# Two U-product steps behind the last scores instead of one early and one ahead of them

## Chip, cores and metric

The kernel runs on one core of a Trainium2 chip. The metric is the device time of one execution in microseconds (us). The engines are TensorE (PE, its weight loads PEld), VectorE (DVE), ScalarE (ACT), GpSimd (POOL) and SyncE (SP, which issues most transfers).

## The reference

One layer of a hybrid backbone for 512 latent tokens of width 1024: a Fourier and recurrent mixer, then the PEER retrieval, which is where the change lies. Every token makes 8 heads x 2 queries, scores 128 sub-keys with each, takes the 16 best of each half, the 16 best of their sums, and uses those experts' rows of two tables of 16384 rows, U and V.

```python
q = (xc @ w_q).reshape(T, PEER_HEADS, 2, PEER_KEY_HALF)
s = jnp.einsum('thpd,hpkd->thpk', q, sub_keys).astype(jnp.float32)
s1, i1 = lax.top_k(s[:, :, 0], PEER_TOPK)
s2, i2 = lax.top_k(s[:, :, 1], PEER_TOPK)
...
sc, pos = lax.top_k(cand, PEER_TOPK)
...
act = jax.nn.gelu(jnp.einsum('thkd,td->thk', u, xc).astype(jnp.float32))
return jnp.einsum('thk,thkd->td', (g * act).astype(xc.dtype), v_tab[idx])
```

## The kernel before

For 352 of the 512 tokens the kernel does not gather rows. It multiplies all of U with the tokens (dense), and later weighs and multiplies with all of V. The products of U come in **steps** of 128 experts (`steps_a`): one step splits a weight tile (ACT makes `whi`, POOL or DVE makes `wlo`), issues 24 matmuls of 128x352 into `ps_pa`, and lets ACT apply the GELU into `act`. A load of 1 MB feeds two steps, and a spill (`Ad<-act`) takes four away. The first 40 steps (numbered 0 to 39 here) are **spilled** ones: their order is that of one generator, and code in the query phase calls `next(spilled)` wherever it wants one more step there, so the calls fix how many steps stand at each place.

The query phase has 16 **blocks** (8 heads x 2 halves). Block k issues 24 matmuls of 128x512 for the query into `ps_ps`, splits the result (`qhi` on ACT, `qlo` on DVE), and then issues the **scores** of the block before it, k - 1: 8 small matmuls (L777, L778) against the split keys `kp` (hi on ACT, lo on POOL), copies on ACT, an addition on POOL (L781), and on DVE the search for the 16 best (`top16`, L764 to L769). After every second block DVE also forms sums of candidates (L792, L794) and searches them. The scores of block 15 come last, behind the loop.

Behind that stands a chain: softmax on DVE and ACT, conversion of positions and indices (`PH`, `IH`), transposes on PE (L884), two gathers by table lookup (`gather_idx`: L897, L900 and L893 on PE, L902 on DVE), with a step after every fourth term, 8 in all. Then come 22 chunks of one-hot products (L958 to L971) with one step each. 10 + 8 + 22 = 40. In the rest of the kernel PE works through the other U groups and all of V.

The tile framework schedules: it builds each engine's queue from the program order and its own cost model, so a step's matmuls may stand earlier than its call. Each engine then works through its queue in order. Weight buffers of the steps (`whi`, `wlo`) are double, so the split of step s + 2 waits for the matmuls of step s.

Of the kernel before, what the change touches and what calls it, by code (L numbers as in the profile page):

```python
# [51 lines left out]
def build(tc, xT, ctxT, c2t, vecs, wm, wu, wf, wg, wgate, wo, wq, keys, u, v, urow, vrow,  # L52
# [12 lines left out]
    def act(o, i, f, bias=None, scale=None, **kw):  # L65
        if bias is not None:
            kw["bias"] = bias
        if scale is not None:
            kw["scale"] = scale
        return S.activation(o, i, f, **kw)  # L70
# [37 lines left out]
    def pst(tag="ps", n=512, dt=F32):  # L108
        return psum.tile([P, n], dt, tag=tag, name="ps_" + tag, bufs={"ps": 5, "pm": 1, "pa": 2}[tag])

    def load(ap, st="", cuts=1):
        t = raws.tile([P, 2048], F32, tag="raw" + st, name="raw")
        n = 2048 // cuts
        for c in range(cuts):
            nc.sync.dma_start(t[:, c * n:(c + 1) * n], ap[:, c * n:(c + 1) * n])
        return t
# [4 lines left out]
    def split(dst, src, lo_eng=None):  # L121
        act(dst[0], src, AF.Copy)
        lo_ins[0] = (lo_eng or V).tensor_tensor(dst[1], src, dst[0].bitcast(F32), op=ALU.subtract).ins  # L123
        return dst

    def split_w(raw, h, lo_eng=None, st=""):
        return split((wspl.tile([P, 1024], F32R, tag="whi" + st, name="whi"),
                      wspl.tile([P, 1024], F32R, tag="wlo" + st, name="wlo")),
                     raw[:, h * 1024:(h + 1) * 1024], lo_eng)

    def mm3(ps, a, b, start, stop):
        PE.matmul(ps, a[0], b[0], start=start, stop=False)  # L132
        PE.matmul(ps, a[0], b[1], start=False, stop=False)  # L133
        PE.matmul(ps, a[1], b[0], start=False, stop=stop)  # L134

    def cut(pair, sl):
        return pair[0][:, sl], pair[1][:, sl]
# [625 lines left out]
    def top16(src, n, vals, idx):  # L763
        V.max(vals[:, 0:8], src)  # L764
        V.max_index(idx[:, 0:8], vals[:, 0:8], src)
        rest = qp.tile([P, n], F32, tag=f"rest{n}", name="rest")
        V.match_replace(rest, vals[:, 0:8], src, -3.4e38)
        V.max(vals[:, 8:16], rest)
        V.max_index(idx[:, 8:16], vals[:, 8:16], rest)  # L769

    def scores(h, p, kp, qT):
        sc = qp.tile([P, T], F32, tag="sc", name="sc")
        for b in range(2):
            ps = pst().rearrange("p (t c) -> p t c", t=2)
            for t in range(2):
                a = cut(qT, slice((2 * b + t) * P, (2 * b + t + 1) * P))
                PE.matmul(ps[:, t], a[0], kp[:, p].rearrange("p c k -> p (c k)"), start=True, stop=False)  # L777
                PE.matmul(ps[:, t, :P], a[1], kp[:, p, 0], start=False, stop=True)  # L778
            sc2 = qp.tile([P, 2, 256], F32, tag="sc2", name="sc2")
            act(sc2, ps, AF.Copy)  # L780
            G.tensor_tensor(sc[:, b * 256:(b + 1) * 256].rearrange("p (t k) -> p t k", t=2),  # L781
                            sc2[:, :, :P], sc2[:, :, P:], op=ALU.add)
        for t4 in range(4):
            top16(sc[:, t4 * P:(t4 + 1) * P], P, M[:, t4, p, h], I[:, t4, p, h])
        if p == 0:
            return
        cand = qp.tile([P, 4, NCAND], F32, tag="cand", name="cand")
        s1 = M[:, :, 0, h]
        s2 = M[:, :, 1, h]
        for a in range(8):  # L790
            n = ROWLEN[a]
            V.tensor_tensor(cand[:, :, START[a]:START[a] + n], s2[:, :, 0:n],  # L792
                            s1[:, :, a:a + 1].to_broadcast([P, 4, n]), op=ALU.add)
        V.tensor_tensor(cand[:, :, 42:50], s1[:, :, 8:16], s2[:, :, 0:1].to_broadcast([P, 4, 8]), op=ALU.add)  # L794
        for t4 in range(4):
            top16(cand[:, t4], NCAND, SC[:, t4, h], PO[:, t4, h])
# [7 lines left out]
    def steps_a(g, lo_eng, done):  # L804

        for w in range(JG // 2):
            raw = load(u[g * (JG // 2) + w], "U" if lo_eng else turn(w))
            for h in range(2):
                wp = split_w(raw, h, lo_by[0] if lo_eng else None, "U" if lo_eng else turn(h))
                ps = pst("pa")  # L810
                for d in range(ND):
                    mm3(ps[:, :TD], cut(wp, slice(d * P, (d + 1) * P)), cut(h2[d], slice(TG, T)),
                        d == 0, d == ND - 1)
                if w % 2 == 0 and h == 0:
                    at = act_tile()
                act(at[:, (2 * w + h) % 4], ps[:, :TD], AF.Gelu_apprx_tanh)
                if w % 2 and h:
                    done(g, w // 2, at)
                yield
# [7 lines left out]
    spilled = itertools.chain.from_iterable(steps_a(g, G, spill) for g in range(NSP))  # L827

    late = None
    for h in range(8):  # L830
        raw = load(wq[h]) if h else None
        kraw = qp.tile([P, 256], F32, tag="kraw", name="kraw")
        nc.sync.dma_start(kraw, keys[h])
        kp = qp.tile([P, 2, 2, P], F32R, tag="kp", name="kp")
        split((kp[:, :, 0], kp[:, :, 1]), kraw.rearrange("p (s k) -> p s k", s=2), G)
        for p in range(2):
            wp = split_w(raw, p, G) if h else wpq[p]
            ps = pst()
            for d in range(ND):
                mm3(ps, cut(wp, slice(d * P, (d + 1) * P)), h2[d], d == 0, d == ND - 1)  # L840
            qT = split((qp.tile([P, T], F32R, tag="qhi", name="qhi"),
                        qp.tile([P, T], F32R, tag="qlo", name="qlo")), ps)
            if late:
                scores(*late)
            if p or h == 0:
                next(spilled)
            late = (h, p, kp, qT)
    next(spilled)
    scores(*late)


    SCv = SC.rearrange("p a h k -> p (a h) k")
# [452 lines left out]
```

## Time and profile before

| | |
|---|---|
| median of 3 runs | 1470.51 us (1467.47 to 1471.3) |
| profiled execution | 1468.34 us, its span 1466.6 us |
| mean granted clock of TensorE | 0.977 of full speed |
| query phase with its first transposes | 251.4 to 413.2 us |
| gathers | 413.2 to 453 us |
| one-hot chunks on PE | 466.9 to 587.9 us |
| products with U, V and row gathers | 600 us to the end |

All stretches below are in us from the span's start. Where an engine's busy time equals a stretch it was never without an instruction there.

### The profile page before, as it was taken

Reading aid. Unit: us, or ns where it says so; the run is one execution under the profiler, and the core shown is the slowest. Engines: PE = TensorE matmul, PEld = TensorE weight load, DVE = VectorE, ACT = ScalarE, POOL = GpSimd, SP = SyncE. Lnnn points to the kernel's source line nnn. Section 1 sums busy time; section 2 is a strip of 40 time slices with the busy share of each in tenths; the row PEclk is TensorE's granted clock in tenths of the full one; section 3 lists DMA queues with packets and bytes.
Section 4 is the critical chain, followed back from the end, with each engine's and each line's share of the span. In section 5 each row is a group of like instructions: output and inputs, shape, how many; then the busy total and the mean of one; then the engine's idle time right before and its main releaser. Section 6 shows DMA issues by size and latency. Waiting matters only on the chain. (4 is left out here: it accounts for less than half of the span.)

```text
span 1466.6 us, 22575 instructions
## 1 busy us (share of the span) xinstructions
PE 1388.5 (95%) x8569; PEld 1286.3 (88%) x8569; DVE 1235.2 (84%) x2184; ACT 613.3 (42%) x881; POOL 680.4 (46%) x462
## 2 busy tenths in 40 slices
PE   6897998999989999999999999999999999899995
PEld 2776765888969999999999999999999999899995
DVE  5577875599986999498998979998898989999973
ACT  4467633434334566533333432424334343243351
POOL 0034163666520000465766746675675766544412
PEclk8899999999999999999999999999999999999998
DMA  8333446331225999999999998999999999999911
GB/s 339 157 115 143 171 174 238 134 114 62 105 79 187 311 293 328 359 380 367 402 358 415 355 373 342 414 382 376 397 369 369 399 348 415 399 410 401 391 39 58
DMA packets 130190, 420.61 MB, mean 287 GB/s; under 512 B 10401, under 2 KB 59809, under 8 KB 106017
## 3 DMA queue, kind: packets, MB, share of 16 engines
q1 hardware_dynamic: 83520, 251.03, 45.9%
q0 software_dynamic: 46560, 168.14, 29.7%
q8 instruction: 67, 1.10, 0.3%
q14 instruction: 43, 0.34, 0.1%
HBM read 385.41 MB, written 33.69 MB: 286 GB/s over the span
## 5 line engine op out<-in xcount | busy, mean ns | idle before, releaser
L70 ACT ACTIVATE whi<-raw 128x1024 fp32r<-128x1024 f32 x296 | 312.8, 1060 | 601.8 <-PE ps_pa L133 301.9
L123 DVE TENSOR_TENSOR wlo<-raw,whi 128x1024 fp32r<-128x1024 f32 x264 | 326.3, 1238 | 44.9 <-ACT whi L70 42.1
L132 PE MATMUL ps_pa<-h2h,whi 128*128 128x352 f32 x1024 | 335.7, 328 | 4.0 <-ACT act L70 4.0
L134 PE MATMUL ps_pa<-h2h,wlo 128*128 128x352 f32 x1024 | 333.6, 326 | 0.3 <-DVE wlo L123 0.3
L133 PE MATMUL ps_pa<-h2l,whi 128*128 128x352 f32 x1024 | 333.2, 325 | 0.0
L1089 POOL DMA_INDIRECT row<-vrow,eidx x128 | 192.8, 1506 | 130.1 <-DVE oacc L1110 100.6
L1089 POOL DMA_INDIRECT row<-urow,eidx x128 | 196.7, 1537 | 120.1 <-DVE row L1096 67.2
L133 PE MATMUL ps_ps<-wl,whi 128*128 128x352 f32 x640 | 207.5, 324 | 0.0
L134 PE MATMUL ps_ps<-wh,wlo 128*128 128x352 f32 x640 | 206.9, 323 | 0.0
L132 PE MATMUL ps_ps<-wh,whi 128*128 128x352 f32 x640 | 206.4, 322 | 0.0
L132 PEld LDWEIGHTS ps_pa<-h2h,whi 128*128 128x128 f32 x1024 | 193.3, 189 | 6.2 <-ACT act L70 4.9
L134 PEld LDWEIGHTS ps_pa<-h2h,wlo 128*128 128x128 f32 x1024 | 193.1, 189 | 1.6 <-DVE wlo L123 0.6
L133 PEld LDWEIGHTS ps_pa<-h2l,whi 128*128 128x128 f32 x1024 | 193.3, 189 | 1.1
L1096 DVE SCALAR_TENSOR_TENSOR row<-row,hrow 128x1024 f32<-128x1024 f32 x128 | 153.6, 1219 | 31.1 <-DMA row<-urow,eidx 30.9
L1110 DVE SCALAR_TENSOR_TENSOR oacc<-row,gw,oacc 128x1024 f32<-128x1024 f32 x127 | 162.4, 1279 | 11.5 <-DMA row<-vrow,eidx 11.1
L133 PEld LDWEIGHTS ps_ps<-wl,whi 128*128 128x128 f32 x640 | 120.3, 188 | 0.0
L134 PEld LDWEIGHTS ps_ps<-wh,wlo 128*128 128x128 f32 x640 | 120.3, 188 | 0.0
L132 PEld LDWEIGHTS ps_ps<-wh,whi 128*128 128x128 f32 x640 | 120.3, 188 | 0.0
L123 POOL TENSOR_TENSOR wlo<-raw,whi 128x1024 fp32r<-128x1024 f32 x32 | 76.6, 2395 | 86.9 <-ACT whi L70 60.0
L133 PE MATMUL ps_pa<-wl,whi 128*128 128x352 f32 x256 | 83.0, 324 | 0.0
L134 PE MATMUL ps_pa<-wh,wlo 128*128 128x352 f32 x256 | 82.7, 323 | 0.0
L132 PE MATMUL ps_pa<-wh,whi 128*128 128x352 f32 x256 | 82.5, 322 | 0.0
(299 smaller groups left out, 2611.7 us busy)
## 6 DMA issues: line engine op xcount, KB each, us to landing
raw<-u SPq DMA_DIRECT2D x64, 1024.0 KB, 7.8
raw<-v SPq DMA_DIRECT2D x64, 1024.0 KB, 8.3
raw<-wm SPq DMA_DIRECT2D x24, 1024.0 KB, 6.1
Gd<-stg SPq DMA_DIRECT2D x22, 1024.0 KB, 6.9
gt<-Gd SPq DMA_DIRECT2D x16, 1408.0 KB, 10.3
raw<-wq SPq DMA_DIRECT2D x8, 1024.0 KB, 4.8
Ad<-act SPq DMA_DIRECT2D x10, 704.0 KB, 5.2
act<-Ad SPq DMA_DIRECT2D x10, 704.0 KB, 6.9
```

The source lines that it names most:

```text
L70: return S.activation(o, i, f, **kw)
L123: lo_ins[0] = (lo_eng or V).tensor_tensor(dst[1], src, dst[0].bitcast(F32), op=ALU.subtract).ins
L132: PE.matmul(ps, a[0], b[0], start=start, stop=False)
L133: PE.matmul(ps, a[0], b[1], start=False, stop=False)
L134: PE.matmul(ps, a[1], b[0], start=False, stop=stop)
L1089: G.indirect_dma_start(out=t, out_offset=None, in_=tab, in_offset=bass.IndirectOffsetOnAxis(ap=e[:, s:s + 1], axis=0))
L1096: ins = V.scalar_tensor_tensor(t, t, 1.0, hr, op0=ALU.mult, op1=ALU.mult, accum_out=dt[:, s:s + 1])
L1110: ins = V.scalar_tensor_tensor(o, t, g[:, s:s + 1], o, op0=ALU.mult, op1=ALU.add)
```

## The change

The call after block 0 goes, and the last two calls stand behind the scores of block 15, where there was one call ahead of them. Blocks still issue one step per head, ten steps are still called by the end of the phase, and everything behind it is unchanged in the code. So step 0 is called after block 1 instead of block 0, step k (1 to 8) one call later, and step 8 and step 9 last.

```diff
             if late:
                 scores(*late)
-            if p or h == 0:
+            if p:
                 next(spilled)
             late = (h, p, kp, qT)
+    scores(*late)
     next(spilled)
-    scores(*late)
+    next(spilled)
```

How it moves instructions on the engines is shown at three places.

On PE, at the first scores (`ps_ps_1983` and `ps_ps_2045` or `ps_ps_2012` are the queries of blocks 0 and 1, `ps_pa` is a step). Before, ahead of the first scores, the tail of step 0 and then 23 matmuls of block 1:

```order
L134 MATMUL ps_ps_1983<-h2h7_1940,wlo_1814 128x512
L132 MATMUL ps_pa_2018<-h2h5_1928,whi_2014 128x352
...
L134 MATMUL ps_pa_2018<-h2h7_1940,wlo_2015 128x352
L133 MATMUL ps_ps_2045<-h2l0_1899,whi_1817 128x512
...
L134 MATMUL ps_ps_2045<-h2h7_1940,wlo_1818 128x512
L777 MATMUL ps_ps_2075<-kp_1980,qhi_2008 128x256
```

Now the queries of blocks 0 and 1 run into each other, the scores follow at once, and step 0 stands behind them:

```order
L134 MATMUL ps_ps_1983<-h2h7_1940,wlo_1814 128x512
L134 MATMUL ps_ps_2012<-h2h3_1916,wlo_1818 128x512
...
L134 MATMUL ps_ps_2012<-h2h7_1940,wlo_1818 128x512
L777 MATMUL ps_ps_2042<-kp_1980,qhi_2008 128x256
...
L133 MATMUL ps_pa_2088<-h2l0_1899,whi_2084 128x352
```

23 of step 0's 24 matmuls moved behind the first scores.

On POOL, at the same place (`wlo` of `raw_2012`, `raw_2082` and `raw_2334` are steps, of `raw_2145` and `raw_2115` blocks 2 and 3). Before:

```order
L716 DMA eyeR_1895<-eye 128x128
L123 TENSOR_TENSOR wlo_2153<-raw_2145,whi_2152 128x1024
L123 TENSOR_TENSOR wlo_2337<-raw_2334,whi_2336 128x1024
L123 TENSOR_TENSOR kp_1980<-kraw_1978,kp_1980 128x2x128
L123 TENSOR_TENSOR kp_2149<-kraw_2147,kp_2149 128x2x128
```

Now:

```order
L716 DMA eyeR_1895<-eye 128x128
L123 TENSOR_TENSOR wlo_2123<-raw_2115,whi_2122 128x1024
L123 TENSOR_TENSOR kp_1980<-kraw_1978,kp_1980 128x2x128
L123 TENSOR_TENSOR kp_2119<-kraw_2117,kp_2119 128x2x128
L123 TENSOR_TENSOR wlo_2231<-raw_2115,whi_2230 128x1024
```

One split instead of two stands ahead of the low part of the keys, `kp`, for which the first scores wait.

On ACT, at the end of the phase, where every step has one `act` row (`sc2` are the copies of scores). Before:

```order
L70 ACTIVATE sc2_3622<-ps_ps_3617 128x512
L70 ACTIVATE sc2_3630<-ps_ps_3625 128x512
L70 ACTIVATE whi_3866<-raw_3864 128x1024
L70 ACTIVATE act_3688<-ps_pa_3663 128x352
L70 ACTIVATE whi_3916<-raw_3864 128x1024
L70 ACTIVATE act_3688<-ps_pa_3694 128x352
L70 ACTIVATE sc2_3726<-ps_ps_3721 128x512
L70 ACTIVATE sc2_3734<-ps_ps_3729 128x512
L70 ACTIVATE whi_3969<-raw_3967 128x1024
L70 ACTIVATE act_3688<-ps_pa_3870 128x352
L70 ACTIVATE whi_4020<-raw_3967 128x1024
L70 ACTIVATE act_3688<-ps_pa_3920 128x352
```

Now:

```order
L70 ACTIVATE sc2_3591<-ps_ps_3586 128x512
L70 ACTIVATE sc2_3599<-ps_ps_3594 128x512
L70 ACTIVATE whi_3765<-raw_3732 128x1024
L70 ACTIVATE act_2995<-ps_pa_3630 128x352
L70 ACTIVATE sc2_3663<-ps_ps_3658 128x512
L70 ACTIVATE sc2_3671<-ps_ps_3666 128x512
L70 ACTIVATE whi_3866<-raw_3864 128x1024
L70 ACTIVATE act_2995<-ps_pa_3738 128x352
L70 ACTIVATE whi_3916<-raw_3864 128x1024
L70 ACTIVATE act_2995<-ps_pa_3769 128x352
```

Between the scores of blocks 14 and 15 stands one step (7), where two stood (8 and 9). Behind the scores of block 15 there were steps 10 and 11, and now there are 8 and 9. In PE's queue 300 step matmuls stood ahead of the first transpose (L884): steps 0 to 11 and 12 matmuls of step 12. Now it is 253: steps 0 to 9 and 13 of step 10. From the transposes of the gathers' results (L927) on, the order on PE is the same in both, so that the 47 matmuls stand between L884 and there. On DVE the split `qlo` of block 15's query keeps its place in the queue.

## Rows read from the trace of the kernel before

**Rows 1.** The page: busy us of each engine (share of the span) and instructions.
```profile
PE 1388.5 (95%) x8569; PEld 1286.3 (88%) x8569; DVE 1235.2 (84%) x2184; ACT 613.3 (42%) x881; POOL 680.4 (46%) x462
```

**Rows 2.** Stretches: length, then busy us of each engine; behind them the granted clock.
```profile
core 0: us, PE busy (x) PEld busy (x) DVE busy (x) ACT busy (x) POOL busy (x), PEclk, DMA share, GB/s
251.36:256.48 5.12, 5.12 (x12) 4.01 (x13) 5.12 (x9) 3.19 (x5) 0.00 (x0) 0.50 0.05 8
...
283.50:406.28 122.78, 122.78 (x663) 108.95 (x661) 121.61 (x786) 48.95 (x79) 74.81 (x57) 1.00 0.26 94
406.28:413.18 6.90, 0.00 (x1) 0.01 (x1) 6.77 (x40) 1.09 (x2) 1.50 (x1) 0.78 0.67 256
413.18:416.90 3.72, 3.72 (x21) 3.72 (x22) 3.14 (x9) 3.12 (x5) 0.00 (x0) 0.50 0.02 4
...
420.50:453.00 32.50, 32.50 (x182) 23.48 (x179) 25.02 (x44) 8.80 (x14) 8.22 (x4) 1.00 0.24 87
453.00:467.00 14.00, 14.00 (x90) 13.68 (x89) 8.31 (x11) 4.66 (x8) 0.00 (x0) 1.00 0.68 236
467.00:587.00 120.00, 119.85 (x1159) 112.15 (x1158) 119.97 (x106) 71.99 (x126) 0.00 (x0) 1.00 0.99 301
```

**Rows 3.** Waits of PE, 240 to 600 us: in total, times, longest.
```profile
PE ps_ps L884 <- DVE PH L872: 6.9, 1, 6.9
```

**Rows 4.** Waits of DVE, 284 to 412.5 us.
```profile
DVE M L764 <- POOL sc L781: 0.4, 1, 0.4
```

**Rows 5.** Timeline of PE ahead of its hole: start, duration, instruction.
```profile
405.80 0.32 PE L133 MATMUL ps_pa<-h2l,whi 128*128 128x352 f32 x1
405.96 0.32 PE L134 MATMUL ps_pa<-h2h,wlo 128*128 128x352 f32 x1
```

**Rows 6.** Timeline of PE around the first scores and at the second.
```profile
268.83 0.28 PE L777 MATMUL ps_ps<-kp,qhi 128*128 128x256 f32 x1
...
269.70 0.38 PE L132 MATMUL ps_pa<-h2h,whi 128*128 128x352 f32 x1
...
279.18 0.28 PE L777 MATMUL ps_ps<-kp,qhi 128*128 128x256 f32 x1
```

**Rows 7.** Timeline of POOL, 258 to 284 us.
```profile
263.13 4.76 POOL L123 TENSOR_TENSOR wlo<-raw,whi 128x1024 fp32r<-128x1024 f32 x2 [12.71 <-ACT whi L70]
267.85 1.43 POOL L123 TENSOR_TENSOR kp<-kraw,kp 128x256 fp32r<-128x256 f32 x2
```

**Rows 8.** Timeline of DVE at the second search for the best.
```profile
283.48 0.49 DVE L764 MAX8 M<-sc 128x8 f32<-128x128 f32 x2 [2.01 <-POOL sc L781]
```

**Rows 9.** Timeline of PE at step 8 and the last scores.
```profile
387.85 0.38 PE L132 MATMUL ps_pa<-h2h,whi 128*128 128x352 f32 x1
...
395.58 0.28 PE L777 MATMUL ps_ps<-kp,qhi 128*128 128x256 f32 x1
```

**Rows 10.** Timeline of DVE: the last query's split.
```profile
394.74 0.68 DVE L123 TENSOR_TENSOR qlo<-ps_ps,qhi 128x512 fp32r<-128x512 f32 x1
```

**Rows 11.** DVE's groups of 389.5 to 392, then of 404.5 to 408.3 us: count, busy, mean ns.
```profile
L792 DVE TENSOR_TENSOR cand<-M 128x8 f32<-128x8 f32 (+5 forms) x8 | 1.0, 174 | 0.0
...
L792 DVE TENSOR_TENSOR cand<-M 128x8 f32<-128x8 f32 (+5 forms) x8 | 3.0, 428 | 0.0
```

**Rows 12.** Timeline of DVE: the last round of additions begins.
```profile
404.78 0.28 DVE L792 TENSOR_TENSOR cand<-M 128x32 f32<-128x32 f32 x2
```

**Rows 13.** Timeline of POOL, 404.5 to 409 us.
```profile
405.43 2.35 POOL L123 TENSOR_TENSOR wlo<-raw,whi 128x1024 fp32r<-128x1024 f32 x1 [1.44 <-ACT whi L70]
```

**Rows 14.** The page: issues of U loads, KB each, us to landing.
```profile
raw<-u SPq DMA_DIRECT2D x64, 1024.0 KB, 7.8
```

**Rows 15.** Timeline of ACT ahead of the first one-hot product.
```profile
459.94 1.06 ACT L70 ACTIVATE whi<-raw 128x1024 fp32r<-128x1024 f32 x1 [2.43 <-PE ps_pa L133]
```

**Rows 16.** Timeline of DVE at the first one-hot product.
```profile
461.03 1.23 DVE L123 TENSOR_TENSOR wlo<-raw,whi 128x1024 fp32r<-128x1024 f32 x1 [1.55 <-ACT whi L70]
462.18 1.22 DVE L958 TENSOR_TENSOR X<-io,i1T 128x2048 f16<-128x2048 f16 x1
```

## The prediction

> **What bounds the kernel now.** The page comes first: PE is busy for 95% of the span and DVE for 84% [rows 1], so an average does not tell which of them sets the pace where the change lies. The table of stretches does. From the second scores to the end of the query phase PE is busy for all of 122.78 us, and DVE for 121.61 [rows 2]. DVE's list of waits has 0.4 us in that time [rows 4]. Both are full, and each feeds the other: DVE waits for no scores because it is behind, PE for no split query. Then comes a hole: PE has nothing for 6.90 us, which its waits put down to `PH`, the last positions that DVE finds [rows 2, 3]. After that PE is without a break again, through the gathers (32.50 of 32.50 us) and up to the first one-hot products (14.00 of 14.00) [rows 2]. In the one-hot chunks DVE sets the pace (119.97 of 120.00), but its first one-hot product stands in its queue behind the split of a step at 461.03, which waited for ACT at 459.94, which waited for PE to free a weight buffer [rows 15, 16]. So the start of that stage too is PE's.
>
> What the reader is to take from this: from the query phase on, PE's amount of work is fixed (40 steps, 16 blocks, the same lookups and chunks), and PE has few holes. The change can win or lose by what it does to PE's idle time, and nearly by that alone.
>
> **The change part by part.** First the unit. Step matmuls start 0.16 us apart [rows 5], so a step is 24 x 0.16 = 3.84 us of PE. The 8 score matmuls take 269.70 - 268.83 = 0.87 us until the next may start [rows 6].
>
> *The step that leaves the start.* 23 of its matmuls stood ahead of the first scores, at 268.83. Without them PE has block 1's query done 3.7 us earlier, at about 265.1. But the scores also need the low part of the keys from POOL. Before, POOL made two splits in 4.76 us from 263.13 on and then the two keys in 1.43 us [rows 7]. Now one split stands ahead: 263.13 + 2.4 + 0.7 = 266.2, and the scores start at about 266.3, which is 2.5 us earlier, with PE idle for 1.2 us. The second scores, behind 23 instead of 24 step matmuls, come at 279.18 - 2.65 = 276.5. DVE got their sums at 283.48 [rows 8] and has no pause worth the name from there to `PH`, so its whole search ends 2.65 us earlier, and the first transpose moves from 413.18 to 410.5. This shift is the least known term. Its lower bound is 0.1 us (POOL works in the old order: 2.4 us more), its upper bound 3.8 us (the keys wait for nothing). I take 2.65, since POOL's queue as built shows one split ahead.
>
> *The steps that leave the end.* Ahead of the first transpose stand 253 step matmuls instead of 300. The other 47 stand behind it, where PE has no idle time to put them in [rows 2, 3]: 47 x 0.16 = 7.5 us.
>
> *Where PE stands idle instead.* Step 8 began at 387.85, the last scores followed at 395.58, and the split of the last query was done by DVE at 394.74 + 0.68 = 395.42 [rows 9, 10]. PE had two steps to pass the time until then. Now it has one: it starts step 7 at 387.85 - 2.65 = 385.2, ends it at 389.0, and waits for the split until 392.8. That is an idle time of 3.8 us that was not there. What is queued behind the waiting scores on PE are just the two steps that were to fill the hole. The scores take 0.9 us, so the steps run from 393.8 on: 61 matmuls, 9.8 us, to 403.6. From there to 410.5 PE is idle again, 6.9 us, as long as before. The two steps behind the last scores thus take no time from the hole, and a second one opens ahead of them.
>
> *What else a step issues.* ACT (48.95 of 122.78 us) and POOL (74.81) are not full [rows 2]. A load of U takes 7.8 us [rows 14] and goes into one of two buffers, each for two steps, so that it is issued at least two steps ahead, 30 us and more in this phase; on SP it now stands behind one more load of queries and keys. Spills move with their step, and nobody waits for them before V. These parts cost nothing; a late load would cost up to 7.8 us once.
>
> *The sum.* -2.65 (start) + 7.5 (behind the transposes) = +4.9 us. The idle times say the same: 1.2 + 3.8 + (6.9 - 6.9) = 5.0, the same to the rounding. On the profiled execution's 1468.34 us (span 1466.6) that is 1473.2. The median of the runs shown lies 2.2 us above that execution, so the measured time should be about 1475 us, 0.33% slower. A measurement of this kernel can tell about 0.3% (4.4 us) from no change, so the forecast lies close to that line.
>
> **The skill against the trace.** Nine small additions form DVE's candidates (eight of L792, one of L794). The eight take 1.0 us when POOL is idle, and 3.0 us in the last round, which begins at 404.78 and has POOL's split beside it from 405.43 to 407.78 [rows 11 to 13]. So 2.0 us of the chain to `PH` come from a step's split. The Trainium skill (SBUF — State Buffer, Who interferes with whom) states the rule: the two engines share a port pair as an exclusive lock, and the one that comes second is blocked for the whole instruction. The trace agrees. By my times the additions begin at 402.1 and POOL's split of step 11 at 402.7, behind the end of step 9 at 401.5 and 1.1 us of ACT: 0.6 us apart, as before. If the split came about 1 us later the chain would escape; that is a rival below.
>
> **The rivals.**
>
> *A. POOL misses the last additions.* `PH` is ready 2.0 us earlier, and the sum is 4.9 - 2.0 = +2.9: 1473 us. For it: the order on POOL and PE around the last scores is new, and a later step 9 suffices. Against it: every time that I worked out moves by the same 2.65 us.
>
> *B. The clock.* Behind each of its long waits PE ran at half its clock, 1.2 GHz: for 5.12 us from 251.36 on and for 3.72 us from 413.18 on [rows 2]. Half of the stretch is lost, 2.6 and 1.9 us. I left this term as it was. If the hole ahead of the transposes no longer brings it, the sum is +3.0; if it lasts as long as the first, +5.6. A half-clock stretch after the new wait would fall into steps 8 and 9 and be swallowed by the hole. With the lower bound of the shift (0.1 us) the sum is +7.4, with the two together +8.1: 1478.6 us.
>
> *C. PE's surplus is hidden, the other side.* If DVE's chain of lookups set the pace behind the transposes, the 47 matmuls would fit into PE's spare time, and all would move by the earlier start alone: -2.65 us, 1468 us, with the upper bound of the shift and no half clock -5.7, 1465 us. It decides as soon as PE has 4.9 us of spare time between 413 and 467 us. For it: DVE is busy for 25.02 of 32.50 us there, more than a bystander, and its lookups are a chain. Against it: PE shows no idle time in that stretch at all, while DVE does.
>
> *D. The steps fill the hole after all.* If the last split did not hold PE up (a DVE that is 3.8 us earlier there), steps 8 and 9 would only end earlier, at 399.9, and the hole would be 10.6 us: the time is the same as forecast, since `PH` does not move with it. It tells where the idle time lies, not how long the kernel takes.
>
> **How the numbers follow.** The forecast with its two places of the idle time (D included): 0.50, of which two thirds lie above the 4.4 us line. B's upper side and the small shift: 0.15, all above. A or no half clock: 0.20, below the line. C: 0.15, about half of it faster by over 0.3%. So slower by over 0.3%: 0.33 + 0.15 = 0.48. Within 0.3%: 0.17 + 0.20 + 0.07 = 0.44. Faster: 0.08. The predicted time is 1475 us. The range goes down to 1469, which leaves out most of C, and up to 1479, B with both bounds; the forecast's own range, with the spread of the medians, is 1472 to 1478.
>
> **What the profile after would show.** Right: first scores near 266.3 us and POOL's keys just ahead; a wait of PE of some 4 us for `qlo` at the last scores, and one of about 7 us for `PH` near 410; the first one-hot products on PE (466.9 before) near 472; the stages behind it moved by the same 5 us. Wrong: first scores at 265 or 268; the last eight additions of candidates back at 1.0 us; one-hot products that start at 466 or sooner, by which PE would have had spare time that its rows do not show; or a later stage that gives the shift back.

## The result

| | before | changed |
|---|---|---|
| median, first measurement | 1467.92 us (1464.96 to 1471.3, 7 runs) | 1474.98 us (1472.19 to 1482.21, 7 runs) |
| median, second measurement | 1469.2 us (1460.86 to 1477.65, 30 runs) | 1471.9 us (1467.22 to 1477.43, 12 runs) |
| profiled execution, its span | 1468.34 us, 1466.6 us | 1472.19 us, 1470.4 us |

The ratio of changed to before, with its 95% interval, was 1.0057 [1.0037, 1.0078] in the first measurement and 1.0028 [1.0009, 1.0047] in the second (it is not the quotient of the medians): the changed kernel is slower by 0.3 to 0.6%, and the intervals overlap between 1.0037 and 1.0047, 5.4 to 6.9 us. The 0.33% of the forecast lie inside the second interval and just below the first.

PE's waits of the changed kernel from 240 to 610 us answer to [rows 3] (in total, times, longest; lines from 849 on are one higher; three that both kernels have, for `h2h` ahead of the phase, at L1066 and at L244, are left out):

```profile
...
PE ps_ps L885 <- DVE PH L873: 3.7, 1, 3.7
PE ps_ps L778 <- DVE qlo L123: 3.4, 1, 3.4
...
PE ps_ps L777 <- POOL kp L123: 1.1, 1, 1.1
PE ps_pm L894 <- DVE lk L903: 0.9, 1, 0.9
```

One wait of 6.9 us became four of 9.1 us together. The new ones for the keys and for the last query are where the forecast put them. The old one, for `PH`, has nearly halved, which was not forecast, and neither was the one for `lk`, a looked-up term of a gather that DVE makes for PE. The stretches, as in [rows 2]:

```profile
core 0: us, PE busy (x) PEld busy (x) DVE busy (x) ACT busy (x) POOL busy (x), PEclk, DMA share, GB/s
252.18:258.20 6.02, 6.02 (x15) 4.65 (x16) 6.02 (x10) 3.24 (x5) 0.00 (x0) 0.50 0.02 4
394.15:398.10 3.95, 3.95 (x17) 3.95 (x18) 3.95 (x30) 1.20 (x2) 1.46 (x2) 0.57 0.83 291
398.10:406.54 8.44, 8.44 (x53) 8.15 (x51) 8.41 (x57) 3.54 (x5) 3.41 (x2) 1.00 0.00 1
406.54:410.25 3.71, 0.00 (x2) 0.01 (x1) 3.58 (x27) 0.93 (x2) 1.54 (x1) 1.00 0.28 60
410.25:414.00 3.75, 3.75 (x31) 3.60 (x32) 3.38 (x9) 3.56 (x7) 0.00 (x0) 1.00 0.52 221
417.00:471.00 54.00, 53.00 (x306) 44.41 (x306) 34.42 (x55) 15.50 (x24) 12.33 (x6) 1.00 0.41 148
```

Behind the wait for the last query (390.71 to 394.15) the granted clock is 0.57, a mix of the levels 1.2 and 2.4 GHz: 3.95 x 0.43 = 1.7 us are lost, and steps 8 and 9 (with 13 matmuls of step 10) end at 406.54 instead of 404.4 (the forecast's 403.6, moved by the 0.8 us by which this execution entered the phase later). Another 0.5 us of that is a wait that ended later, at 394.15 instead of 393.6. Behind the transposes the clock is now 1.00, where it was 0.50.

The last additions on DVE (eight of L792, 402.5 to 405.6 us) answer to [rows 11], POOL's splits beside them to [rows 13]:

```profile
L792 DVE TENSOR_TENSOR cand<-M 128x8 f32<-128x8 f32 (+5 forms) x8 | 1.5, 239 | 0.0
```

```profile
401.63 2.40 POOL L123 TENSOR_TENSOR wlo<-raw,whi 128x1024 fp32r<-128x1024 f32 x1 [4.67 <-ACT whi L70]
405.53 2.55 POOL L123 TENSOR_TENSOR wlo<-raw,whi 128x1024 fp32r<-128x1024 f32 x1 [1.49 <-ACT whi L70]
```

The additions take 1.5 us instead of 3.0. The second split, due at 402.7 + 0.8 = 403.5 by the forecast, came at 405.53, when they were over. This is rival A, at 1.5 of its 2.0 us: the split ahead, which ended at 404.03, still held up the first two, which began at 403.33 and took 0.85 us, where they took 0.28 before [rows 12].

PE's timeline gives the places by which all kernels are compared below: the first query matmul, the first scores, the wait for the last query, the first transpose, the first one-hot product.

```profile
252.18 1.22 PE L132 MATMUL ps_ps<-h2h,whi 128*128 128x512 f32 x2 [5.81 <-ACT h2h L70]
...
267.56 0.39 PE L777 MATMUL ps_ps<-kp,qhi 128*128 128x256 f32 x1 [1.06 <-POOL kp L123]
...
394.15 0.33 PE L778 MATMUL ps_ps<-kp,qlo 128*128 128x128 f32 x1 [3.44 <-DVE qlo L123]
...
410.25 0.40 PE L885 MATMUL ps_ps<-selt,PH 128*128 128x128 f16 x4 [3.71 <-DVE PH L873]
...
471.03 0.39 PE L969 MATMUL ps_ps<-Y,X 128*128 128x128 f16 x4
```

Every execution enters the query phase at another time (251.36 before, 252.18 here), so the table counts from the first query matmul of each. The last column is the first matmul on `hrow`, near 1425 us.

| kernel | scores | transpose | one-hot | `hrow` |
|---|---|---|---|---|
| before | 17.47 | 161.82 | 215.49 | 1170.90 |
| changed | 15.38 | 158.07 | 218.85 | 1172.39 |
| again | 14.91 | 157.57 | 218.86 | 1174.52 |
| start alone | 15.36 | 159.66 | 218.71 | 1174.37 |
| end alone | 17.75 | 160.47 | 220.43 | 1177.19 |
| four more steps | 17.39 | 161.79 | 232.28 | 1177.96 |
| POOL beside the sums | 15.00 | 161.37 | 223.03 | 1176.11 |
| keys on DVE | 14.81 | 157.49 | 219.58 | 1175.05 |
| steps of the gather | 17.43 | 161.84 | 216.54 | 1171.94 |
| GH late | 17.50 | 161.86 | 217.46 | 1173.33 |
| split held back | 16.77 | 159.05 | 213.31 | 1170.24 |

At the one-hot chunks the change costs 218.85 - 215.49 = 3.4 us, where 4.9 were forecast. The last column moves by 2.1 us between two executions of the same code (changed, again), so a difference of 1 or 2 us is read at the one-hot column and not from a median. Each kernel but the changed one has one profile.

### The profile page after: what moved, and what is told of

The parts are those of the page before. It is cut to its first block, busy times and chain, and to the rows that moved or that the text cites. A ratio compares the mean times of both kernels' runs of the same rounds, so it can differ in the third digit from the quotient of the medians.

```text
span 1470.4 us, 22580 instructions
## 1 busy us (share of the span) xinstructions
PE 1393.3 (95%) x8569; PEld 1290.9 (88%) x8569; DVE 1235.2 (84%) x2184; ACT 613.9 (42%) x881; POOL 685.7 (47%) x462
## 3 DMA queue, kind: packets, MB, share of 16 engines
q1 hardware_dynamic: 83520, 251.03, 45.9%
## 5 line engine op out<-in xcount | busy, mean ns | idle before, releaser
L1090 POOL DMA_INDIRECT row<-vrow,eidx x128 | 195.9, 1530 | 130.5 <-DVE oacc L1111 96.7
```

The lines of the kernel that those rows point to most:

```text
L1090: G.indirect_dma_start(out=t, out_offset=None, in_=tab, in_offset=bass.IndirectOffsetOnAxis(ap=e[:, s:s + 1], axis=0))
```

## The experiments

**The changed kernel again**, no edit, to see whether what the profile shows is stable.

> The changed kernel once more, unaltered. Theory (TensorE's work is fixed from the query phase on, so the time moves by the change of its idle time): first scores near 267, waits of 1.1 us for the keys, 3.4 us for the last query's split and 3.5 to 7 us for the positions, one-hot products 3 to 5 us later than before, and 3 to 5 us more at the end, 0.2 to 0.35%. Rival (the long stage behind 600 us has a second cost, since the times seen so far lie at 1472 to 1475 and at 1480 to 1482): 0.5% or more, and a profile in which the shift grows by 3 us or more behind 600 us.

Measured: the second row of medians above. The three waits are the same to 0.01 us, and so is the shift at the one-hot product (3.37 us). The rival did not come out: the shift of 3.4 us at the one-hot product is 3.6 us at `hrow`. Two stretches of its profile, at the transposes and at the start of the phase:

```profile
407.82:412.20 4.38, 4.38 (x26) 4.13 (x26) 3.99 (x10) 3.50 (x7) 0.00 (x0) 0.61 0.48 201
250.25:255.20 4.95, 4.95 (x12) 3.86 (x13) 4.95 (x8) 3.02 (x5) 0.00 (x0) 0.50 0.03 5
```

Here the half clock behind the transposes is back (4.38 x 0.39 = 1.7 us lost), at a hole of the same 3.71 us. In exchange the 0.9 us that PE waited for `lk` are gone. Two operations show why, first in the changed kernel's first execution, then in this one (`bm` is a mask that DVE makes for the second gather, in its queue among the lookups of the first):

```profile
415.11 2.46 DVE L920 TENSOR_SCALAR bm<-posT 128x512 f16<-128x512 f16 x1
415.06 2.37 POOL L123 TENSOR_TENSOR wlo<-raw,whi 128x1024 fp32r<-128x1024 f32 x1 [6.97 <-ACT whi L70]
...
412.68 0.29 DVE L920 TENSOR_SCALAR bm<-posT 128x512 f16<-128x512 f16 x1
413.32 2.37 POOL L123 TENSOR_TENSOR wlo<-raw,whi 128x1024 fp32r<-128x1024 f32 x1 [7.66 <-ACT whi L70]
```

At the full clock the next step's split came 4.8 us behind the first transpose, at half the clock 5.5; the earlier one held `bm` up for 2.2 us, and PE had to wait for the lookup behind it. So the clock there isn't decided by the hole's length alone, and of the 1.7 us that it costs 0.5 are left at the one-hot product (60.8 and 61.3 us behind the first transpose). At the start the stretch at 0.50 is 4.95 us long, 6.02 in the first execution and 5.12 before. Half of these differences is lost or gained there, compared with the kernel before: with it the scores of both executions come 2.5 us earlier (17.47 - 15.38 + 0.45 and 17.47 - 14.91 - 0.09).

**The start alone, the end alone.** Each leaves the other half as before.

```diff
 # start alone
-            if p or h == 0:
+            if p:
                 next(spilled)
...
     next(spilled)
     scores(*late)
+    next(spilled)
```

```diff
 # end alone
             if p or h == 0:
                 next(spilled)
...
-    next(spilled)
     scores(*late)
+    next(spilled)
```

> Only the start of the change: step 0 leaves the place behind block 0 and goes behind the last scores; one step stays ahead of them. 276 step matmuls stand ahead of the first transpose (300 before, 253 in the changed kernel), and two steps between the last two scores. Theory: search 2.6 us earlier, 24 x 0.16 = 3.8 us more behind the transposes, no wait for the last query's split, so +1.2 us (0.1%). Rival (the early step is what hid the start, so its removal is the whole loss): +4 us or more. Rival (DVE's chain sets the pace, steps behind the transposes are free): -2.6 us.

> Only the end of the change: the early step stays, the step ahead of the last scores goes behind them. 277 step matmuls stand ahead of the first transpose, one step between the last two scores. Theory: first scores at 268.8 as before, a wait of about 3.5 us for the last query's split, 23 x 0.16 = 3.7 us more behind the transposes, so +3.7 us (0.25%). Rival (the start is the whole loss): 0. Rival (steps behind the transposes are free): 0.

Measured: 1473.01 us, ratio 1.0017 [0.9995, 1.0039], and 1472.7 us, 1.0032 [1.001, 1.0054]. PE's waits from 250 to 475 us, of the start alone:

```profile
PE ps_ps L884 <- DVE PH L872: 6.9, 1, 6.9
...
PE ps_pm L893 <- DVE lk L902: 1.4, 1, 1.4
PE ps_ps L777 <- POOL kp L123: 1.1, 1, 1.1
```

and of the end alone:

```profile
PE ps_ps L884 <- DVE PH L872: 3.7, 1, 3.7
PE ps_ps L778 <- DVE qlo L123: 3.4, 1, 3.4
PE ps_pm L893 <- DVE lk L902: 1.4, 1, 1.4
```

The waits part as forecast: the one for the keys belongs to the start, that for the last query and the halved hole to the end. But each half moves the one-hot product by more than forecast, 3.2 and 4.9 us, and the two don't add up to 3.4. Behind the transposes stand 24 and 23 more step matmuls (3.8 and 3.7 us), and the way from there to the one-hot product grew by 5.4 and 6.3 us: in both, 1.4 us are a wait for the lookups on DVE, which neither before nor the second execution of the changed kernel has. It comes from `bm` beside a step's split once more, here of the start alone (of the end alone 2.38 us beside a split from 433.46 on):

```profile
433.28 2.37 DVE L919 TENSOR_SCALAR bm<-posT 128x512 f16<-128x512 f16 x1
433.04 2.46 POOL L123 TENSOR_TENSOR wlo<-raw,whi 128x1024 fp32r<-128x1024 f32 x1 [3.96 <-ACT whi L70]
```

The rest of the end's is a longer stretch at half clock behind the transposes, 5.70 us instead of 3.72.

**Four more steps behind the last scores**, to fill the hole of the kernel before; the calls then leave four fewer for the one-hot chunks.

```diff
     next(spilled)
     scores(*late)
+    next(spilled)
+    next(spilled)
+    next(spilled)
+    next(spilled)
```

> The kernel before with four more steps behind the last scores (the last chunks of one-hot products then have no step beside them). 336 step matmuls stand ahead of the first transpose instead of 300: 36 x 0.16 = 5.8 us of the hole of 6.9 us are filled. Theory: the wait for the positions shrinks to about 1 us and the time falls by 5.8 us, by up to 2 us more if no half clock follows (0.4 to 0.5%). Rival (idle time there is given back later, since DVE sets the pace of the one-hot chunks): 0 to -1 us.

Measured: 1477.27 us, 1.0081 [1.0049, 1.0113], slower where the theory had it faster and the rival unchanged. The hole for `PH` did shrink as forecast. PE's waits from 405 to 425 us, DVE's softmax, and POOL at that time:

```profile
PE ps_ps L884 <- DVE GH L863: 5.9, 1, 5.9
PE ps_ps L884 <- DVE PH L872: 1.2, 1, 1.2
```

```profile
413.68 2.77 DVE L859 SCALAR_TENSOR_TENSOR EX<-EX,Z 128x512 f32<-128x512 f32 x1
416.49 2.45 DVE L863 CAST GH<-EX 128x512 f16<-128x512 f32 x1
```

```profile
413.57 2.34 POOL L123 TENSOR_TENSOR wlo<-raw,whi 128x1024 fp32r<-128x1024 f32 x1 [6.69 <-ACT whi L70]
416.29 2.37 POOL L123 TENSOR_TENSOR wlo<-raw,whi 128x1024 fp32r<-128x1024 f32 x1 [0.38 <-ACT whi L70]
```

The hole moved to the next transposes, those of `GH`: the matmuls that had stood between the two groups were now ahead of both. And the added steps' splits on POOL stood beside two operations of the softmax on DVE, which take 0.68 and 0.42 us in the kernel before. PE did four steps more ahead of the one-hot chunks (15.4 us; the one-hot product came 16.8 us later). The chunks were no shorter: from their first product to their last 120.9 us in both kernels, with 474 step matmuls among them, 472 before. The four steps that the calls left out there were made up by steps of the groups behind the 40, which moved up in PE's queue (ahead of the chunks stood 336 + 283, and 40 steps have 960). So only PE's later work was less, and 7.1 of the 16.8 us are left at `hrow`. A further wait of 4.85 us near 700 us I have not followed up.

**POOL beside the sums**: the changed kernel with an operation on POOL that nobody needs.

```diff
+        if h == 7:
+            pad = qp.tile([P, 64, 16], F32, name="pad", bufs=1)
+            m = M[:, 3, 1, 7][:, None].to_broadcast([P, 64, 16])
+            G.tensor_tensor(pad, m, m, op=ALU.subtract)
         cand = qp.tile([P, 4, NCAND], F32, tag="cand", name="cand")
```

> The changed kernel with one more operation on POOL, a tensor_tensor of 128x1024 that waits for the last search of block 15, so that it stands beside the last nine additions (L792, L794). In the changed kernel the eight of L792 took 1.5 us there instead of 3.0 before, because POOL's split came 0.5 us behind them. Theory (POOL beside them is what holds the additions up): they take 3.3 us or more again, PH and the first transpose come 1.5 to 2.0 us later, PE's wait for PH is 5.2 to 5.7 us instead of 3.7, the first one-hot product on PE stands 220.4 us behind the first query matmul instead of 218.9, and the time is 1.5 us longer. Rival (the additions were shorter for another reason): they stay at 1.5 us and nothing moves.

Measured: 1476.83 us, 1.0052 [1.0027, 1.0077]. The additions (L796 here), POOL, and PE's wait:

```profile
L796 DVE TENSOR_TENSOR cand<-M 128x8 f32<-128x8 f32 (+5 forms) x8 | 5.2, 699 | 0.0
```

```profile
403.51 1.89 POOL L790 TENSOR_TENSOR pad<-M 128x1024 f32<-128x1024 f32 x1 [0.42 <-DVE M L768]
405.36 2.34 POOL L123 TENSOR_TENSOR wlo<-raw,whi 128x1024 fp32r<-128x1024 f32 x1
```

```profile
PE ps_ps L889 <- DVE PH L877: 7.4, 1, 7.4
```

The theory's direction, at twice its size: the additions grew by 3.7 us, PE's wait by 3.7, and the one-hot product came 4.2 us later. The added operation held one addition up, and as it delayed the others, the split that the changed kernel escapes caught the next one, for 2.32 us.

**Keys on DVE**: the changed kernel with the low part of the first head's keys made by DVE.

```diff
-        split((kp[:, :, 0], kp[:, :, 1]), kraw.rearrange("p (s k) -> p s k", s=2), G)
+        split((kp[:, :, 0], kp[:, :, 1]), kraw.rearrange("p (s k) -> p s k", s=2), G if h else V)
```

> The changed kernel with the low part of the first head's keys made by DVE instead of POOL. Theory: PE's wait of 1.06 us for kp at the first scores goes, the first scores stand 13.9 us behind the first query matmul (14.9 to 15.4 before this edit), all of DVE's search moves by as much, PE's wait for qlo stays 3.4 us and that for PH 3.7 us, the first one-hot product is 1.0 us nearer to the first query matmul (217.9), and the time falls by 1.0 us. Rival (the first scores are held by something else, the split of the query on DVE): they move by less than 0.4 us and the wait is only renamed.

Measured: 1472.7 us, 1.0012 [0.9993, 1.003]. The rival came out: PE waits 0.66 us instead of 1.06, now for DVE, and the one-hot product came 0.7 us later, not 1.0 earlier (the stretch at half clock behind the transposes was 5.1 us long). DVE makes the keys behind the split of the first query, and beside POOL's split of 264.52 to 266.92:

```profile
264.94 0.69 DVE L123 TENSOR_TENSOR qlo<-ps_ps,qhi 128x512 fp32r<-128x512 f32 x1 [3.23 <-ACT qhi L70]
265.55 1.65 DVE L123 TENSOR_TENSOR kp<-kraw,kp 128x256 fp32r<-128x256 f32 x1
```

**Steps of the gather behind the last scores**, and its control. As with the four more steps, but the four come from the first gather, and the transposes of `GH` and `GL` stand behind that gather, with the softmax multiplications that feed them (a scale that depends on the gather's result keeps them there).

```diff
     scores(*late)
+    next(spilled)
+    next(spilled)
+    next(spilled)
+    next(spilled)
...
-    gather_idx(i1T, r1T, 0, [(None, 0)] + [(1, START[a]) for a in range(1, 16)], posT, ALU.is_ge)
+    gather_idx(i1T, r1T, 0, [(None, 0)] + [(1, START[a]) for a in range(1, 16)], posT, ALU.is_ge, ())
+    turned(ghT, GH)
+    turned(glT, GL)
```

> The kernel before with four more steps behind the last scores, taken from the first gather, which issues none now, so that 18 steps stand ahead of the one-hot chunks as before; the softmax multiplications and the transposes of GH and GL stand behind the first gather. Theory (time follows PE's idle time): 336 step matmuls stand ahead of the first transpose, PE's wait for PH falls from 6.9 to 1.2 us, nothing waits for GH, the first one-hot product is 5.7 us nearer to the first query matmul (209.8 instead of 215.5), up to 1.9 us more if the half clock behind the transposes goes, and the time is 1463.5 us, 0.4% faster. Rivals: the lookups, with fewer steps between them, wait for DVE and take 3 us or more back; or a later stage gives it back and the end does not move.

> The control of the run before: only the softmax multiplications and the transposes of GH and GL stand behind the first gather, with no step moved by a call. Theory: PE's wait for PH stays at 6.9 us, the first one-hot product stays 215.5 us (within 1) behind the first query matmul, the time stays that of the kernel before. Rival (DVE's softmax held the gathers up): the first one-hot product comes 1 us or more earlier without any filling.

Measured: 1473.32 us, 1.0016 [0.9999, 1.0033], and for the control, without the four steps, 1472.58 us, 1.0026 [1.0011, 1.0042]. PE's waits of the first from 405 to 475 us, and two of its stretches:

```profile
PE ps_pa L132 <- ACT act L70: 2.2, 1, 2.2
PE ps_pm L882 <- DVE lk L891: 2.1, 1, 2.1
PE ps_ps L870 <- DVE PH L859: 1.2, 1, 1.2
```

```profile
417.30:424.30 7.00, 4.73 (x24) 3.55 (x25) 3.23 (x5) 5.72 (x9) 4.72 (x2) 0.76 0.00 0
444.38:448.20 3.82, 3.82 (x11) 1.81 (x11) 3.02 (x5) 0.44 (x1) 0.00 (x0) 0.55 0.33 133
```

The hole is filled (1.2 us), and what was won came back behind it: 2.2 us on a step, which waited for the `act` of an earlier one (on ACT that stood behind the softmax, a split and the load of a function table, to 420.30; the step's own `wlo` was ready only at 420.94), 2.1 us on the lookups (DVE had an operation of 0.43 us held for 2.48 beside POOL's split, at 438.69), and 1.7 us lost to the clock behind each, 3.82 x 0.45 in the second. Together 1.2 + 2.2 + 2.1 + 3.4 = 8.9 us, where the kernel before has 6.9 + 1.9 = 8.8. The first rival holds for the lookups' share, 2.1 + 1.7 us; the rest is the step's. With 36 fewer step matmuls the way from the first transpose to the one-hot product took 54.7 us, before 53.7. In the control it grew by 1.9 us, 1.4 of them a wait for `GH` at its new place, so that the one-hot product, forecast within 1 us, came 2.0 us later; the softmax had not held the gathers up. Against the control, which has the same order but for the steps, the filling gained 0.9 us at the one-hot product (216.54, 217.46), of 5.7 forecast.

**The split held back**: the kernel before, with a tiny operation on POOL that reads the last sums, ahead of POOL's next split.

```diff
+        if h == 7:
+            pad = qp.tile([P, 8], F32, name="pad", bufs=1)
+            G.tensor_tensor(pad, cand[:, 3, 42:50], cand[:, 3, 42:50], op=ALU.subtract)
```

> The kernel before with a small operation on POOL (128x8) that reads the last sums of candidates and so holds POOL's next split back until the last additions are done. Theory (that split alone makes them long, and what stands behind the first transpose follows it): the eight of L792 take 1.0 us instead of 3.0, the first transpose comes 2.0 us earlier against the first query matmul (159.8 us behind it instead of 161.8), PE's wait for PH is 4.9 us, the first one-hot product stands 213.5 us behind the first query matmul instead of 215.5, and the time is 2 us shorter (0.14%, less than the rounds can tell for sure). Rival (the split that comes later is late for its step): the first transpose is earlier but the first one-hot product is not.

Measured: 1468.58 us, 1.0 [0.9985, 1.0015], beside 1467.32 for the kernel before. The additions, POOL, PE's wait:

```profile
L792 DVE TENSOR_TENSOR cand<-M 128x8 f32<-128x8 f32 (+5 forms) x8 | 0.9, 172 | 0.0
```

```profile
407.46 0.58 POOL L797 TENSOR_TENSOR pad<-cand 128x8 f32<-128x8 f32 x1 [2.21 <-DVE cand L794]
408.01 2.34 POOL L123 TENSOR_TENSOR wlo<-raw,whi 128x1024 fp32r<-128x1024 f32 x1
```

```profile
PE ps_ps L887 <- DVE PH L875: 4.8, 1, 4.8
```

The additions are 2.1 us shorter and the wait is 4.8 us, as forecast; the first transpose is 2.8 us earlier and the one-hot product 2.2 us. Of both, 0.7 us were gained at the start of the phase, where the scores were early by as much, so the edit is worth 2.1 us at the transpose and 1.5 at the one-hot product (the stretch at half clock behind the transposes was 5.0 us instead of 3.7). The rival falls. The gain is too small for the medians to show, and at `hrow` only 0.7 us are left, no more than the start gave.

## Why the forecast was right, and where it was not

It was slower, as forecast, and the time fits: 1474.98 us beside 1475. That it fits so closely is luck. The forecast counted 4.9 us up from 1470.51, the median of three runs; the median of all seven is 1467.92, the medians lie 7.1 us apart in the first measurement and 2.7 in the second. The sum behind the forecast, read at the one-hot product, was 1.5 us too high:

| term | forecast | changed | again |
|---|---|---|---|
| first scores, from the first query matmul | -2.5 | -2.1 | -2.6 |
| first transpose, from the first query matmul | -2.7 | -3.8 | -4.3 |
| from the first transpose to the one-hot product | +7.5 | +7.1 | +7.6 |
| one-hot product | +4.9 | +3.4 | +3.4 |

*The start* was right: the keys on POOL hold the first scores, PE waits 1.06 us (1.2 forecast), and the search on DVE moves with the scores. The keys are not alone in it: with them made on DVE, PE's wait is only 0.4 us shorter.

*The 47 matmuls behind the transposes* cost about what they were forecast to, 7.1 and 7.6 us. In the first execution that is a sum of things that were not forecast, too: 1.9 us for a half clock that didn't come and 1.0 of idle time, most of it the wait for `lk`, leave 8.0 for the matmuls. Rival C falls in this direction: PE had no spare time to hide them. The run with steps of the gather shows the other direction: with 36 fewer, 0.9 us was won against its control, since a step's wait for ACT and DVE's lookups come next. This suggests that the kernel before stands where the two are about equal, which the rows of [rows 2], PE full for 32.50 of 32.50 us, could not tell.

*Idle time nearly alone* was too narrow a rule. Up to the one-hot product PE's idle time grew by 2.3 us in the first execution and by 1.4 in the second, what it lost at the lower clock by 0.3 and 1.5 us; 0.8 and 0.5 us of the shift are in neither.

*The wait for the last query* was right, 3.44 us (3.8 forecast), and so was the statement that the two steps behind it fill nothing that had been empty before them.

*"0.6 us apart, as before"* is the step that failed, and with it the hole of 6.9 us. I had the half clock behind the new wait swallowed by the hole, and rival A set off by a late step 9, and didn't join the two: the half clock is what makes step 9 late. It lost 1.7 us, with the later end of the wait the steps ended 2.1 us later than forecast, POOL's split came 2.0 us later, the additions were 1.5 us shorter, and `PH` was ready 1.1 us earlier than forecast. So the hole was 6.9 - 2.1 - 1.1 = 3.7 us. Between the first addition and POOL's split lie 2.2 us in all four profiles that have the wait and put nothing new on POOL there (changed, again, end alone, keys on DVE), and 0.6 us before and in the start alone, which lack it: the 1.6 us between them are nearly the 1.7 us of the clock. The end alone shows the same 3.7 us and its transposes 1.35 us earlier; the start alone keeps 6.9 us. That POOL beside the additions does it is shown twice: an operation put there again cost 3.7 us, the split held back in the kernel before gave 2.1. That the half clock alone made the split late rests on the times in the traces; no run has the wait without it. Rival A, which the forecast priced at +2.9 us, is thus what came, at +3.4.

The Trainium skill (SBUF — State Buffer, Who interferes with whom) says that a DVE operation with two inputs in SBUF and a POOL operation that reads SBUF shut each other out, that an operation in a two-port mode, which a cast or a `tensor_scalar` can enter, contends with POOL as well, and that one with a single input outside these modes isn't touched. The traces agree on DVE's side: additions, the multiplication of the softmax (2.77 us instead of 0.68), the cast (2.45 instead of 0.42) and `bm`, a `tensor_scalar` (2.37 to 2.46 instead of 0.29), were held; the searches were not, as the changed kernel's groups show ahead of POOL's split (399 to 401.6 us) and beside it (401.65 to 403.3):

```profile
L765 DVE FIND_INDEX8 I<-M,sc 128x8 uint32<-128x128 f32 x3 | 0.9, 286 | 0.0
...
L765 DVE FIND_INDEX8 I<-M,sc 128x8 uint32<-128x128 f32 x2 | 0.6, 286 | 0.0
```

Of the difference in time, 3.8 us lie between the two spans. At the one-hot product it is 3.4 us against the phase's start plus 0.8 that came ahead of the phase; 1.9 of these 4.2 are gone at `hrow`, and 1.5 us come behind it. These last 1.5 don't go with the change: behind the first matmul on `hrow` the kernel takes 44.3 us in five of the eleven profiles (before, start alone, end alone, POOL beside the sums, GH late; granted clock 0.83 to 0.86) and 45.7 to 45.9 us in the other six (0.80 or 0.81). Why the first measurement has 7.1 us between the medians and the second 2.7 stays open. Three of the first measurement's seven runs of the changed kernel took 1480 to 1482 us, and three of the end alone 1479 to 1481, which no run of the kernel before did (1477.65 at most); none of these was profiled.

## What to carry to other kernels

A wait that is filled is won only if the next chain is shorter: before work is moved into a hole, look for what the engine would wait for next, and what the moved work's other instructions (here the splits on POOL) stand beside. A wait for DVE can be a wait for POOL: here an addition, a cast or a mask of 0.2 to 0.4 us took up to 2.5 us beside a split. When a new wait is put on TensorE, count the slower clock behind it as a delay of what follows, and ask what that delay lets pass or makes collide. Where a change is worth a few us, compare distances from a common event in the traces; medians of whole runs could not show 2 us.

## What the runs showed of the hardware

Two POOL operations that follow each other each held one DVE addition up: in the run with POOL beside the sums the four additions that began at 403.78 took 4.10 us, while POOL was busy from 403.51 to 407.70, against 0.43 us for the same four in the changed kernel:

```profile
403.78 4.10 DVE L796 TENSOR_TENSOR cand<-M 128x64 f32<-128x64 f32 x4
```

The clock behind a wait was not the same in two executions of one kernel: behind the same hole of 3.71 us it was 1.00 in one and 0.61 over 4.38 us in the other, with the one-hot product at the same distance in both.
